# An encoder layer on one core: where the second part of x is loaded and rounded, and when the last half's seven-product sums are added

## The chip, the cores and the metric

The kernel runs on one core of a Trainium2 chip. A core has five engines that run side by side, each through its own list of instructions in order: TensorE (PE, matrix products into the eight banks of PSUM), VectorE (DVE), ScalarE (ACT), GpSimd (POOL) and SyncE (SP, which here only starts transfers). They wait for each other through semaphores. The metric is the device time of one execution in microseconds; the kernel before has a median of 1289.85 us over 3 runs (1289.42 to 1290.4).

## The reference

One layer over 256 positions of width 2048, in float32: a token mixer of two gated branches, a convolutional gated MLP, a last RMSNorm. What matters here is the first projection and the last one:

```python
def mixer_block(x, g_norm, w_in, ln_g, ln_b, w_s, b_s, rpb, w_branch, w_out):
    h = rms_norm(x, g_norm)
    proj = h @ w_in
...
    merged = g_a * (y_a @ w_branch[:GM_WIDTH]) + g_b * (y_b @ w_branch[GM_WIDTH:])
    return x + merged @ w_out

def conv_ffn(x, g_norm, w_up, conv_k, conv_b, w_down):
    h = rms_norm(x, g_norm)
    up = h @ w_up
...
    gate, val = jnp.split(up, 2, axis=-1)
    return x + (jax.nn.silu(gate) * val) @ w_down
...
        x = conv_ffn(x, norm_ffn[l], w_up[l], conv_k[l], conv_b[l], w_down[l])
    return rms_norm(x, norm_final)
```

with w_in 2048 x 9216, w_up 2048 x 11008 and w_down 5504 x 2048.

## The kernel before

**Products in three parts.** Each operand of a product is split into a rounded high part and the rest: ACT rounds (`whi` for weights, L170), DVE subtracts (`wlo`, L171). A product is then three matmuls, high by high, low by high and high by low (L317, L318, L319 in `triple`).

**Pieces.** The weights are streamed as a list of pieces through one queue of SP. `begin(i)` (L197) stands ahead of the matmuls of piece i: it starts loads up to piece i + 4 (LOAD_AHEAD is 5), runs the tasks that were set for piece i with `at(i, ...)`, and issues the split of pieces up to i + 3 (SPLIT_AHEAD is 3, with four buffers for `whi` and four for `wlo`). In the first nine pieces the tasks come before the splits, later behind them. What stands in the engines' lists, and in which order, follows from this. `preload[i]` holds transfers that are started ahead of the load of piece i.

**The start.** The first product is a `wide` group, v = x @ w_in with 1024 columns: a piece holds 128 rows of the weight, in two halves of 512 columns, and goes with one of the sixteen parts of the transposed x (`xr`, 128 x 256 each, made into high and low by `x_split`, L554). Pieces 0, 1 and 2 go with parts 0, 1 and 6 of x. Before the first weights are there, PE runs WAKE matmuls on a tile of ones (L498), whose result nobody reads. Parts 0 and 1 of x are started on ACT's own queue (L477, L478), everything else on SP's. Piece 0 is loaded and split by halves, and the split of part 1 of x stands between its two halves (L181 to L183).

**The end.** The last product, a @ w_down, is made in two halves of 1024 columns, `g_dn[0]` and `g_dn[1]`, each a `wide` group of 43 pieces (numbered 0 to 42 here within the half). In 13 pairs of pieces a scheme with seven products in place of eight is used; four of its results stand in banks of their own, p1, p5, p6, p7, and the other four banks C belong to the output's blocks (t, c), t the half of the positions and c the 512 columns. The last such pair of the second half are pieces 36 and 37. Behind piece 37 `ev_sums` sets two tasks: `first_half` (one ACT copy, L995, and five DVE additions, L996 to L1000, that make the sums and read the four banks) for piece 38, and `second_half` (three DVE additions, L1003 to L1005, into `x2`, the residual) for piece 39. Piece 38 is done in all four blocks; pieces 39 to 42 are done block by block (L440), so that the first blocks can be finished while PE works on the others. When a block is done, `finish` (L1149) runs: DVE adds it to `x2` (L1114), ACT squares and sums it (L1120), DVE multiplies by the norm's weight (L1160). Behind block (0,0), DVE also adds `x2` into the bank of block (1,1) (L1166), ahead of PE's four pieces for that block. When both blocks of a t are there, DVE and ACT make the inverse root (L1174 to L1178), scale the row block (L1186, L1191) and SP and ACT write it out (L1182).

Of the kernel before, what the change touches and what calls it, by code (L numbers as in the profile page):

```python
# [38 lines left out]

LOAD_AHEAD = 5  # L40
SPLIT_AHEAD = 3
WAKE = 9
V_QUADS, V_ORDER = ((5,), (0, 1, 6, 7, 8, 9, 10, 11, 12, 13, 2, 3, 4, 5, 14, 15))
VA_QUADS, VA_ORDER = ((2, 4, 6), (6, 7, 0, 1, 2, 3, 10, 11, 4, 5, 14, 15, 12, 13, 8, 9))
X_TURN = ((0, 0), (3, 1), (4, 2), (5, 3), (1, 4), (2, 5), (6, 6), (7, 9))
# [33 lines left out]
def trunk_kernel(ctx, tc, x, x_t, vecs, w_in, ln_g, ln_b, w_st, b_s, rpb, w_branch, w_out, w_up, w_down,  # L79
                 norm_final, out):  # L80
    nc = tc.nc
# [77 lines left out]
    def split_to(n):  # L159
        while n_split[0] < min(n, len(pieces)):  # L160
            i = n_split[0]
            n_split[0] += 1
            src, r0, kn, (c0, cn, nb, cs), step = pieces[i]
            w = raw.pop(i)
            h = wpool.tile([128, 2, 512], F32R, name="whi", bufs=SPLIT_AHEAD + 1)
            l = wpool.tile([128, 2, 512], F32R, name="wlo", bufs=SPLIT_AHEAD + 1)
            m = cn * nb

            def part(k):
                nc.scalar.activation(h[:, k, :m], w[:, k, :m], AF.Copy)  # L170
                nc.vector.tensor_sub(l[:, k, :m], w[:, k, :m], h[:, k, :m].bitcast(F32))  # L171

            if i in units:
                part(slice(0, units[i]))
            elif i == 1:
                part(slice(0, 1))
                part(slice(1, 2))
            elif i:
                part(slice(0, kn))
            else:  # L180
                part(slice(0, 1))  # L181
                x_split(1)
                part(slice(1, 2))  # L183
            split_t[i] = (h, l)

    tasks = {}
    preload = {}

    def at(i, f):
        tasks.setdefault(i, []).append(f)  # L190
# [6 lines left out]
    def begin(i):  # L197
        cur[0] = i
        load_to(i + LOAD_AHEAD)
        if i < len(SPLIT_TO):  # L200
            run_tasks(i)
            split_to(SPLIT_TO[i])
        else:
            split_to(i + SPLIT_AHEAD + 1)
            run_tasks(i)
# [78 lines left out]
    def wide(src, row0, order, c0, acts, quads, room, done, sums=None, stored=None, split=None, late=False, lead=4, behind=()):  # L284
        n0 = plan_wide(src, row0, order, c0)
        boxes = {}
        for q in quads:
            i = n0 + 2 * q
            k = order[2 * q]
            units[i], units[i + 1] = 1, 2  # L290
            b = boxes[q] = {}
            ready = split[0].get(k // 2) if split else None
            if stored:
                b["acts"] = {}
                at(i - (ready[0] if ready else lead), lambda b=b, k=k: stored(k // 2, b["acts"]))
            else:
                b["acts"] = sums[k]
            if ready:
                halved.add(i)
                for n, lead in zip(("13", "24"), ready[-2:]):  # L300
                    at(i - lead, lambda b=b, k=k, n=n: split[1](k // 2, b, n))
                continue
            whole[i] = whole[i + 1] = None
            halves = late and q == quads[0]
            at(i - 3, lambda i=i, b=b, halves=halves: weight_sums(i, b, room, halves))
            if halves:
                at(i - 2, lambda b=b: b.pop("rest")())
            at(i - (1 if q in behind else 2), lambda b=b: weight_sums_split(b, room))
        return ("wide", n0, order, acts, quads, boxes, done)
# [160 lines left out]
    def load_xt(k, n, queue=None):  # L470
        c = slice(KD + k * T if k else 0, KD + (k + n) * T)
        (queue or nc.sync).dma_start(xall[:, c], x_t[:, c])
# [2 lines left out]
    gffn = const.tile([128, KD], F32)  # L475
    ck = const.tile([128, 4, 2 * NF], F32)
    load_xt(0, 1, nc.scalar)  # L477
    load_xt(1, 1, nc.scalar)  # L478

    def load_late():  # L480
        nc.sync.dma_start(gffn, vecs[:, :KD])
# [14 lines left out]
    def keep_awake(n):  # L496
        for _ in range(n):
            nc.tensor.matmul(wake, idle[:, :128], idle[:, :512], start=True, stop=True)  # L498

    keep_awake(WAKE)  # L500

# [52 lines left out]
    def x_split(k):  # L554
        a, g = xT[k], gmix[:, k:k + 1]
        if k:
            nc.scalar.activation(a[:, 0, :], xr[:, k], AF.Copy, scale=g)
        else:
            nc.vector.tensor_scalar(a[:, 0, :], xr[:, k], g, None, op0=OP.mult)
        nc.vector.scalar_tensor_tensor(a[:, 1, :], xr[:, k], g, a[:, 0, :].bitcast(F32), op0=OP.mult, op1=OP.subtract)  # L560
# [8 lines left out]
    def first_room(name, dt):  # L569
        return ypool.tile([128, 2, 512], dt, name=f"y{first_rooms.index('t13' if name == 'f' else name)}")  # L570
# [411 lines left out]

    rs = {}

    def ev_sums(j, room):
        def done(P, i):
            x2 = rs["x2"]
            p1, p5, p6, p7 = P
            x11, x12, x21, x22 = (x2[:, t, c * 512:(c + 1) * 512] for t in range(2) for c in (j, j + 1))
            m = {}  # L990

            def first_half():
                ab, cd = room("t13", F32), room("t24", F32)
                m["v"], m["u3"], m["w"] = cd[:, 0], cd[:, 1], ab[:, 0]
                nc.scalar.activation(ab[:, 0], p1, AF.Copy)  # L995
                nc.vector.tensor_add(x11, p1, x11)  # L996
                nc.vector.tensor_sub(ab[:, 1], ab[:, 0], p6)
                nc.vector.tensor_add(m["v"], p5, ab[:, 1])
                nc.vector.tensor_add(m["u3"], p7, ab[:, 1])
                nc.vector.tensor_add(m["w"], p5, m["u3"])  # L1000

            def second_half():
                nc.vector.tensor_sub(x12, x12, m["v"])  # L1003
                nc.vector.tensor_add(x21, x21, m["u3"])
                nc.vector.tensor_sub(x22, x22, m["w"])  # L1005

            at(i + 1, first_half)
            at(i + 2, second_half)
        return done


# [221 lines left out]
    for n, (q, i, j) in enumerate(X_SUMS):  # L1233
        sum_acts_at(i, j, first_sums[2 * q], lambda q=q: q,
                    lambda name, dt, i=i: first_room("s2" if name == "f" and i < 16 else name, dt), f"s{n}", True)
# [17 lines left out]
    def split_read(kept, g, tile_of, queue=nc.gpsimd):  # L1253
        def read(pair, box, n):
            u = box.setdefault("u", [])
            u.append([tile_of(pair, p + n) for p in "hl"])
            for t, src in zip(u[-1], kept[pair, g][n]):
                queue.dma_start(t.bitcast(F32), src)
            if len(u) == 2:
                split_sums(box, u)  # L1260
        return read
# [62 lines left out]
    def out_split_tile(pair, name):  # L1324
        if pair == OUT_SET:
# [3 lines left out]
    t_kept = {}  # L1329
    g_o = [wide(w_o, 0, OUT_ORDER[g], g * 1024, lambda k: mg["mT"][k], OUT_QUADS[g], sums_room,  # L1330
                (ev_sums(2 * g, sums_room), ev_out(g)), m_sums, split=(OUT_SPLIT[g], split_read(t_kept, g, out_split_tile)), late=g == 0) for g in range(2)]
    dram = keep("dram", space=bass.MemoryType.DRAM)
    for n, (pair, g) in enumerate((pair, g) for g in range(2) for pair in OUT_SPLIT[g]):
        t_kept[pair, g] = split_rows("out", pair, g)
        i = g_at[2 * n][1]
# [46 lines left out]
    for n, q in enumerate(OUT_PAIRS):  # L1382
        i = g_m2[0][1] + OUT_SUMS[n]
# [22 lines left out]
    def down_order(g):  # L1406
        free = [p for p in range(NF // 2) if p not in DOWN_PAIRS]
        kept = list(DOWN_PAIRS)
        pairs = [(kept if q in DOWN_QUADS[g] else free).pop(0) for q in range(NF // 2)]
        return tuple(2 * p + kk for p in pairs for kk in range(2)) + (NF - 1,)  # L1410

    g_dn = [wide(w_d, 0, down_order(g), g * 1024, lambda k: ff["a"][k], DOWN_QUADS[g], down_room,
                 (ev_sums(2 * g, down_room), ev_down if g == 0 else finish), stored=stored,
                 split=({p: (6, 6) for p in DOWN_SPLIT}, split_read(d_kept, g, down_split_tile))) for g in range(2)]
    ff["kept"] = {p: dram.tile([128, 2, 512], F32, name=f"sums{p}") for p in DOWN_PAIRS}
    for p, turn in zip(DOWN_SPLIT, DOWN_JOBS):
        for g in range(2):
            d_kept[p, g] = split_rows("down", p, g)
            i = g_up[turn[g]][1]
            split_ahead(w_d, d_kept, lambda: ff["more"], lambda c: "so", nc.gpsimd, p, g, g * 1024, i, range(i + 6, i + 10), (i + 10, i + 12), 0)  # L1420

    first_chunk = X_TURN[1][0]
    preload[2] = [lambda: load_xt(2 * first_chunk, 1)]
    preload[3] = [lambda: load_xt(2 * first_chunk + 1, 1)]
    for n, (c, _) in enumerate(X_TURN[2:]):
        preload.setdefault(n + 4, []).append(lambda c=c: load_xt(2 * c, 2))
    for n, i in enumerate(LOAD_ROWS):
        preload.setdefault(i, []).append(lambda n=n: load_x(512 * n, 512))
    at(0, lambda: x_split(0))
    at(0, lambda: split_to(1))  # L1430
    at(1, lambda: x_split(2 * first_chunk))
    at(1, lambda: split_to(3))
# [165 lines left out]
```

## Time and profile before

| | |
|---|---|
| median of 3 runs | 1289.85 us (1289.42 to 1290.4) |
| the profiled execution's own time | 1290.33 us |
| its span, first to last instruction | 1288.5 us |
| granted TensorE clock, mean over the span | 0.998 |
| DVE busy | 1118.3 us, 87% of the span, 1644 instructions |
| ACT busy | 793.0 us, 62%, 1179 instructions |
| POOL busy | 162.1 us, 13% |
| DMA read and written | 284 GB/s over the span |

Times in a timeline are counted from the span's start. A row gives the start, the duration, the engine, the line, the operation, what it writes and reads, how many such instructions stand in the row, and in brackets how long the engine had been idle before it and what it had waited for. PEld are weight loads into the array, which run beside the matmuls. "SPq" and "ACTq" are the instructions that start transfers. The chain of waits is the sequence of work that ended last, followed back from the end.

### The profile page before, as it was taken

What the parts mean: (1) busy time and instruction counts of PE and PEld (TensorE: products, weight loads), DVE (VectorE), ACT (ScalarE), POOL (GpSimd) and SP (SyncE); (2) the same over time, 40 slices, a digit from 0 to 9 for tenths busy, and PEclk for the clock granted to TensorE, in tenths of its full rate; (3) what the DMA queues carried; (4) which work ended last, traced back from release to release, by engine and by line L of the source; (5) the groups of instructions that cost most, each with busy time, mean ns of one, the idle gap of its engine ahead of it and who ended that gap; (6) DMA issues with size and microseconds to landing.
All of it is one profiled execution on the core that took longest, in us unless ns stands there. A gap on an engine that the chain in (4) does not pass through costs nothing.

```text
span 1288.5 us, 19673 instructions
## 1 busy us (share of the span) xinstructions
PE 1277.2 (99%) x6717; PEld 1088.7 (84%) x6717; DVE 1118.3 (87%) x1644; ACT 793.0 (62%) x1179; POOL 162.1 (13%) x307
## 2 busy tenths in 40 slices
PE   9999999999999999999999999999999999999997
PEld 7888888888887888888888888888888888888885
DVE  7898977777799989996889999998988989979987
ACT  7776575775755655565665666665665656556654
POOL 0003852330000001100001000100000001211210
PEclk9999999999999999999999999999999999999999
DMA  9789889989789977965688789888776859998993
GB/s 364 278 272 284 288 263 345 341 284 321 247 314 360 347 238 262 387 215 179 193 281 286 239 275 304 272 260 291 261 227 219 279 174 359 374 387 321 353 392 132
DMA packets 199893, 369.51 MB, mean 287 GB/s; under 512 B 15984, under 2 KB 124144, under 8 KB 199792
## 3 DMA queue, kind: packets, MB, share of 16 engines
q1 hardware_dynamic: 175472, 286.36, 64.7%
q0 software_dynamic: 23888, 81.23, 17.7%
q8 instruction: 52, 0.85, 0.2%
q10 hardware_dynamic: 432, 0.66, 0.1%
q14 instruction: 49, 0.40, 0.1%
HBM read 320.48 MB, written 45.61 MB: 284 GB/s over the span
## 4 chain that ended last, share of the span: by engine, by line
PE 96%; DVE 2%; DMA 1%; issue 1%; DVEq 0%; ACT 0%; SPq 0%; ACTq 0%
PE bank L222 31%; PE bank L226 16%; PE bank L319 11%; PE bank L317 11%; PE bank L318 11%; PE bank L250 5%; PE bank L251 5%; PE bank L252 5%; DMA wraw<-in_w_down_dram 1%; DVE wlo L171 1%; PE bank L871 0%; PE bank L825 0%; PE bank L498 0%; PE bank L860 0%; PE bank L698 0%
## 5 line engine op out<-in xcount | busy, mean ns | idle before, releaser
L171 DVE TENSOR_TENSOR wlo<-wraw,whi 128x1024 fp32r<-128x1024 f32 (+1 forms) x472 | 537.4, 1152 | 125.0 <-ACT whi L170 74.8
L170 ACT ACTIVATE whi<-wraw 128x1024 fp32r<-128x1024 f32 (+1 forms) x472 | 463.8, 995 | 224.1 <-PE bank L318 65.1
L222 PE MATMUL bank<-h,whi 128*128 128x512 f32 x1760 | 423.3, 391 | 0.0
L222 PEld LDWEIGHTS bank<-h,whi 128*128 128x128 f32 x1760 | 322.7, 188 | 62.1
L226 PEld LDWEIGHTS bank<-h,wlo 128*128 128x128 f32 x1760 | 225.9, 191 | 8.8
L226 PE MATMUL bank<-h,wlo 128*128 128x256 f32 x1760 | 228.6, 283 | 0.0
L1076 ACT ACTIVATE tc<-ta,ck 128x256 f32<-128x256 f32 x86 | 47.1, 595 | 109.8 <-DVE ta L1074 109.8
L319 PE MATMUL bank<-wlo,a 128*128 128x512 f32 x188 | 73.4, 390 | 0.6 <-DVE wlo L171 0.6
L318 PE MATMUL bank<-whi,a 128*128 128x512 f32 x188 | 73.2, 389 | 0.0
L317 PE MATMUL bank<-whi,a 128*128 128x512 f32 x188 | 73.1, 389 | 0.0
L317 PE MATMUL bank<-whi,h 128*128 128x512 f32 x186 | 72.8, 392 | 0.0
L319 PE MATMUL bank<-wlo,h 128*128 128x512 f32 x186 | 72.6, 390 | 0.0
L318 PE MATMUL bank<-whi,h 128*128 128x512 f32 x186 | 72.6, 390 | 0.0
L1079 DVE SCALAR_TENSOR_TENSOR tc<-ta,ck,tc 128x255 f32<-128x255 f32 x86 | 41.4, 482 | 14.4 <-ACT tc L1076 14.4
L250 PE MATMUL bank<-whi,h 128*128 128x512 f32 x128 | 50.3, 393 | 0.0
L250 PE MATMUL bank<-whi,y 128*128 128x512 f32 x128 | 50.3, 393 | 0.0
L251 PE MATMUL bank<-whi,h 128*128 128x512 f32 x128 | 49.8, 389 | 0.0
L251 PE MATMUL bank<-whi,y 128*128 128x512 f32 x128 | 49.8, 389 | 0.0
L252 PE MATMUL bank<-wlo,h 128*128 128x512 f32 x128 | 49.8, 389 | 0.0
L252 PE MATMUL bank<-wlo,y 128*128 128x512 f32 x128 | 49.8, 389 | 0.0
L374 ACT ACTIVATE h<-h 128x1024 fp32r<-128x1024 f32 x36 | 38.1, 1059 | 17.5 <-DVE h L364 12.0
L1308 POOL DMA_DIRECT2D down_h<-so x16 | 8.7, 544 | 311.2 <-ACT tc L1086 184.9
(325 smaller groups left out, 1990.1 us busy)
## 6 DMA issues: line engine op xcount, KB each, us to landing
wraw<-in_w_up_dram SPq DMA_DIRECT2D x336, 256.0 KB, 4.1
wraw<-in_w_in_dram SPq DMA_DIRECT2D x107, 512.0 KB, 6.1
wraw<-in_w_down_dram SPq DMA_DIRECT2D x78, 512.0 KB, 7.5
wraw<-in_w_in_dram SPq DMA_DIRECT2D x70, 256.0 KB, 4.4
wraw<-in_w_branch_dram SPq DMA_DIRECT2D x32, 512.0 KB, 5.3
wraw<-in_w_out_dram SPq DMA_DIRECT2D x28, 512.0 KB, 5.9
h<-sums POOLq DMA_DIRECT2D x18, 512.0 KB, 7.5
tw<-in_w_down_dram POOLq DMA_DIRECT2D x8, 1024.0 KB, 8.9
```

What stands on the lines that cost most here:

```text
L170: nc.scalar.activation(h[:, k, :m], w[:, k, :m], AF.Copy)
L171: nc.vector.tensor_sub(l[:, k, :m], w[:, k, :m], h[:, k, :m].bitcast(F32))
L222: nc.tensor.matmul(p, h[:, k - k0, b * 128:(b + 1) * 128], acts(k), start=k == 0, stop=k == nk - 1)
L226: nc.tensor.matmul(p[:, :T], l[:, k - k0, b * 128:(b + 1) * 128], acts(k)[:, 0, :], start=False, stop=False)
L250: nc.tensor.matmul(p, xh, h[:, kk, :m], start=st, stop=False)
L251: nc.tensor.matmul(p, xl, h[:, kk, :m], start=False, stop=False)
L252: nc.tensor.matmul(p, xh, l[:, kk, :m], start=False, stop=sp)
L317: nc.tensor.matmul(p, xh, h, start=st, stop=False, **kw)
L318: nc.tensor.matmul(p, xl, h, start=False, stop=False, **kw)
L319: nc.tensor.matmul(p, xh, l, start=False, stop=sp, **kw)
L1076: nc.scalar.activation(v, u, AF.Identity, scale=ck[:, 1, ch:ch + 1], bias=ck[:, 3, ch:ch + 1])
L1079: nc.vector.scalar_tensor_tensor(v[:, 1:], u[:, :T - 1], ck[:, 0, ch:ch + 1], v[:, 1:], op0=OP.mult, op1=OP.add)
```

## The change

Four edits. Part 1 of x is no longer started on ACT's queue at the beginning, but on SP's, ahead of the load of piece 1, which is behind the two loads of piece 0. The split of part 1 of x stands behind both halves of piece 0 and no longer between them. PE runs 8 wake matmuls in place of 9. In the second half of the last product, `first_half` and `second_half` are set for one piece later each: 39 and 40 in place of 38 and 39 (`late` is the half's number g, so the first half of the last product stays as it is, and so does the product before it, which uses the default).

```diff
-WAKE = 9
+WAKE = 8
...
                 part(slice(0, 1))
+                part(slice(1, 2))
                 x_split(1)
-                part(slice(1, 2))
...
     load_xt(0, 1, nc.scalar)
-    load_xt(1, 1, nc.scalar)
...
-    def ev_sums(j, room):
+    def ev_sums(j, room, late=0):
...
-            at(i + 1, first_half)
-            at(i + 2, second_half)
+            at(i + 1 + late, first_half)
+            at(i + 2 + late, second_half)
...
-                 (ev_sums(2 * g, down_room), ev_down if g == 0 else finish), stored=stored,
+                 (ev_sums(2 * g, down_room, g), ev_down if g == 0 else finish), stored=stored,
...
+    preload[1] = [lambda: load_xt(1, 1)]
```

From L478 on the changed kernel's lines have numbers that are lower by one, up to its new line near the end.

SP's list of transfers at the start, before the change (`wraw` 128x512 are the halves of piece 0, 128x1024 the later pieces, `xr` the parts of x):

```order
L143 DMA wraw<-in_w_in_dram 128x512 x2
L145 DMA wraw<-in_w_in_dram 128x1024
L472 DMA xr<-in_x_t_dram 128x256
L145 DMA wraw<-in_w_in_dram 128x1024
L472 DMA xr<-in_x_t_dram 128x256
```

and with the change:

```order
L143 DMA wraw<-in_w_in_dram 128x512 x2
L472 DMA xr<-in_x_t_dram 128x256
L145 DMA wraw<-in_w_in_dram 128x1024
L472 DMA xr<-in_x_t_dram 128x256
L145 DMA wraw<-in_w_in_dram 128x1024
L472 DMA xr<-in_x_t_dram 128x256
```

One transfer of x has come in ahead of piece 1, and each later transfer stands one place further back.

ACT's list at the start, before:

```order
L472 DMA xr<-in_x_t_dram 128x272
L472 DMA xr<-in_x_t_dram 128x256
L491 ACT_TABLE_LOAD
L491 ACTIVATE one<-one 128x1
L170 ACTIVATE whi<-wraw 128x512
L557 ACTIVATE h_109<-xr 128x256
L170 ACTIVATE whi<-wraw 128x512 x3
```

and with the change:

```order
L472 DMA xr<-in_x_t_dram 128x272
L490 ACT_TABLE_LOAD
L490 ACTIVATE one<-one 128x1
L170 ACTIVATE whi<-wraw 128x512 x2
L556 ACTIVATE h_107<-xr 128x256
L170 ACTIVATE whi<-wraw 128x512 x2
```

The second half of piece 0 is rounded ahead of part 1 of x (`h_109`, `h_107`), and one transfer less is started here. DVE's list is changed in the same way.

DVE's list at the end, before, from the splits of pieces 38 to 41 to the first block's addition (`x_5315` is the residual `x2`, `h_13182` and `h_13183` the two tiles of the sums):

```order
L171 TENSOR_TENSOR wlo<-wraw,whi 128x1024 x4
L996 TENSOR_TENSOR x_5315<-bank,x_5315 128x512
L997 TENSOR_TENSOR h_13182<-h_13182,bank 128x512
L998 TENSOR_TENSOR h_13183<-bank,h_13182 128x512
L999 TENSOR_TENSOR h_13183<-bank,h_13182 128x512
L1000 TENSOR_TENSOR h_13182<-bank,h_13183 128x512
L171 TENSOR_TENSOR wlo<-wraw,whi 128x1024
L1003 TENSOR_TENSOR x_5315<-x_5315,h_13183 128x512
L1004 TENSOR_TENSOR x_5315<-x_5315,h_13183 128x512
L1005 TENSOR_TENSOR x_5315<-x_5315,h_13182 128x512
L1114 TENSOR_TENSOR x_5315<-bank,x_5315 128x512
```

and with the change:

```order
L171 TENSOR_TENSOR wlo<-wraw,whi 128x1024 x5
L995 TENSOR_TENSOR x_5314<-bank,x_5314 128x512
L996 TENSOR_TENSOR h_13197<-h_13197,bank 128x512
L997 TENSOR_TENSOR h_13198<-bank,h_13197 128x512
L998 TENSOR_TENSOR h_13198<-bank,h_13197 128x512
L999 TENSOR_TENSOR h_13197<-bank,h_13198 128x512
L1002 TENSOR_TENSOR x_5314<-x_5314,h_13198 128x512
L1003 TENSOR_TENSOR x_5314<-x_5314,h_13198 128x512
L1004 TENSOR_TENSOR x_5314<-x_5314,h_13197 128x512
L1113 TENSOR_TENSOR x_5314<-bank,x_5314 128x512
```

The split of the last piece, 42, stood between the two groups of additions; now it is the fifth of the splits, and all eight additions stand behind it. ACT's list changes alike: the rounding of piece 42 now stands ahead of the copy of `first_half`. Nothing else in the lists of DVE, ACT, POOL and SP differs; on PE only the one wake matmul is gone.

## The prediction, made before the changed kernel was run

> **What bounds the kernel now.** I read the busy times first, then the chain of waits, then the timelines of its two ends, since all four edits are there.
>
> ```profile
> PE 1277.2 (99%) x6717; PEld 1088.7 (84%) x6717; DVE 1118.3 (87%) x1644; ACT 793.0 (62%) x1179; POOL 162.1 (13%) x307
> PE 96%; DVE 2%; DMA 1%; issue 1%; DVEq 0%; ACT 0%; SPq 0%; ACTq 0%
> ```
>
> PE is busy for 99% of the span and is 96% of the chain. Between the ends there is nothing that these edits touch, so the whole change is worth what it does in the first 12 us and in the last 27. At the start (PE rows, then the chain's own pieces):
>
> ```profile
> 1.46 4.02 PE L498 MATMUL bank<-h 128*128 128x512 bf16 x9 [1.46 <-DVE one L488]
> 5.06 0.85 PE L317 MATMUL bank<-whi,h 128*128 128x512 f32 x1
> 6.13 0.55 PE L319 MATMUL bank<-wlo,h 128*128 128x512 f32 x1
> 6.52 0.40 PE L317 MATMUL bank<-whi,h 128*128 128x512 f32 x1
> 6.75 0.39 PE L318 MATMUL bank<-whi,h 128*128 128x512 f32 x1
> ...
> 5.47 0.43 PE bank L317
> 5.90 0.43 PE bank L318
> 11.90 0.38 PE bank L319
> ```
>
> The chain runs from the wake matmuls into the product without a gap: at the front PE waits for its own wake work. It works at 0.43 us per matmul until about 6.5 us and at 0.23 afterwards (6.52 to 6.75).
>
> **The wake matmul and the loads.** One wake matmul is 4.02 / 9 = 0.45 us. What the first product needs, and what it waits for a little later (the last row is a stretch of time: busy us of PE, PEld, DVE, ACT and POOL, the granted clock, the DMA engines' busy share, GB/s):
>
> ```profile
> 4.37 0.63 ACT L170 ACTIVATE whi<-wraw 128x512 fp32r<-128x512 f32 x1 [1.21 <-DMA wraw<-in_w_in_dram]
> 4.53 0.35 DVE L559 TENSOR_SCALAR h<-xr 128x256 fp32r<-128x256 f32 x1 [3.12 <-DMA xr<-in_x_t_dram]
> 5.32 0.68 DVE L171 TENSOR_TENSOR wlo<-wraw,whi 128x512 fp32r<-128x512 f32 x1
> 5.99 1.92 ACT L170 ACTIVATE whi<-wraw 128x512 fp32r<-128x512 f32 x3
> 7.21 0.39 PE L317 MATMUL bank<-whi,h 128*128 128x512 f32 x1
> 8.57 0.39 PE L317 MATMUL bank<-whi,h 128*128 128x512 f32 x1
> 9.40 1.06 ACT L170 ACTIVATE whi<-wraw 128x1024 fp32r<-128x1024 f32 x1 [0.74 <-DMA wraw<-in_w_in_dram]
> 10.50 1.23 DVE L171 TENSOR_TENSOR wlo<-wraw,whi 128x1024 fp32r<-128x1024 f32 x1 [1.31 <-ACT whi L170]
> 11.78 0.19 PEld L319 LDWEIGHTS bank<-wlo,h 128*128 128x128 f32 x1 [0.30 <-DVE wlo L171]
> 2.11 0.43 SPq L472 DMA_DIRECT2D xr<-in_x_t_dram  x1
> 5.00:12.00 7.00, 7.00 (x29) 5.34 (x28) 5.45 (x9) 5.12 (x9) 0.00 (x0) 1.00 0.97 361
> ```
>
> With 8 wakes the first L317 could start 0.45 earlier, and its inputs just about allow it (`whi` is there at 4.37 + 0.63 = 5.00, x at 4.53 + 0.35 = 4.88). But the third matmul needs `wlo`, ready at 5.32 + 0.68 = 6.00, and it started at 6.13: PE gains 0.13 us and then waits. DVE's row waited 3.12 us for x part 0, which keeps its own place at the head of ACT's queue, so I do not move 6.00. Next, piece 2: its load lands at 9.40, `wlo` is done at 10.50 + 1.23 = 11.73, and the weight load of the third matmul already waits 0.30 us for it. Whatever PE gains before 11.78 is added to that wait. So what decides is whether piece 2 lands earlier. It stands one transfer later on SP (0.43 us of issue, the row at 2.11), but as many bytes are ahead of it as before, and the engines of DMA are 97% busy from 5 to 12 us at 361 GB/s: the landing is set by bytes. **Head: 0**, between -0.45 (all inputs earlier by the wake) and +0.43 (piece 2 later by the issue); 0 because the row at 11.78 is the one that ends last.
>
> The swapped roundings cost nothing here: the second half of piece 0 is used at 7.21, part 1 of x and piece 1 at 8.57. Before, ACT was done with the second half at 5.99 + 1.92 / 3 = 6.63 and with piece 1 at 5.99 + 1.92 = 7.91; the same four roundings in another order end there too, and part 1 of x lands ahead of piece 1, which follows it in SP's queue. That cover is 0.66 us; beyond it each late microsecond is one of PE's. The bound of +0.43 covers it.
>
> On the same place the Trainium skill speaks against the edit: "Trainium Kernel Development and Optimization", section Key Constraints, says that transfers started from several queues share the same 16 engines, and that only issue time is saved. By that rule the move to SP loses the saved issue, up to the +0.43 of my bound, and wins no bandwidth; the 97% row agrees with shared engines, and no row here shows two queues faster than one.
>
> **The end: the sums behind the last split.** Rows of DVE, ACT and PE:
>
> ```profile
> 1268.15 1.06 ACT L170 ACTIVATE whi<-wraw 128x1024 fp32r<-128x1024 f32 x1 [3.62 <-PE bank L318]
> ...
> 1266.94 0.69 DVE L996 TENSOR_TENSOR x<-bank,x 128x512 f32<-128x512 f32 x1
> 1270.19 1.22 DVE L171 TENSOR_TENSOR wlo<-wraw,whi 128x1024 fp32r<-128x1024 f32 x1
> 1271.32 0.69 DVE L1003 TENSOR_TENSOR x<-x,h 128x512 f32<-128x512 f32 x1
> 1273.13 0.69 DVE L1114 TENSOR_TENSOR x<-bank,x 128x512 f32<-128x512 f32 x1
> 1274.46 0.69 DVE L1166 TENSOR_TENSOR bank<-bank,x 128x512 f32<-128x512 f32 x1
> 1279.14 0.75 DVE L1186 TENSOR_SCALAR x<-x,b 128x1024 f32<-128x1024 f32 x1
> 1280.98 0.21 DVE L1175 TENSOR_SCALAR a<-ss,part 128x1 f32<-128x1 f32 x1 [0.38 <-ACT junk L1120]
> ...
> 1270.44 0.39 PE L318 MATMUL bank<-whi,a 128*128 128x512 f32 x1
> 1271.46 0.50 PE L319 MATMUL bank<-wlo,a 128*128 128x512 f32 x1 [0.63 <-DVE wlo L171]
> 1277.28 0.39 PE L317 MATMUL bank<-whi,a 128*128 128x512 f32 x1
> ```
>
> Before: DVE does the five additions (1266.94 to 1270.19, 3.25 us), then the split of piece 42 (1.13 us until the next starts), the three additions (1271.32 to 1273.13, 1.81), then `finish`. PE could have had its L319 at 1270.44 + 0.23 = 1270.67 and starts it at 1271.46: 0.79 us lost.
>
> Now: the split of piece 42 comes first. It needs the rounding by ACT, and that row waits not for ACT's turn but for PE: a `whi` buffer comes free when piece 38's matmuls are done. So it still ends at 1268.15 + 1.06 = 1269.21. DVE, free at 1266.94, has eight additions queued behind the waiting split and stands idle for 1269.21 - 1266.94 = 2.27 us. Then the split (1.13), 3.25 and 1.81: `finish` begins at 1275.40 where it began at 1273.13, **2.27 later**. The split is done at 1269.21 + 1.22 = 1270.43, ahead of 1270.67: PE's 0.79 us are won, as the edit's form suggests, and PE would start its last block at 1277.28 - 0.79 = 1276.49. But that block waits for L1166, which has x2 added to its bank: before, it ended at 1274.46 + 0.69 = 1275.15, 2.13 us ahead of PE; now at 1277.42, 0.93 behind it. The win is gone there, and PE ends 0.14 us later than before.
>
> From 1273.13 on DVE's list is a chain in which no row waits for PE; its only wait is 0.38 us ahead of L1175, for ACT's squares of the last block. So the first row block's scaling (L1186 at 1279.14) moves by 2.27, and the last block's, after the 0.38, by 1.89. What that does to the end is read from the transfers:
>
> ```profile
> 1279.92 3.73 SPq L1182 DMA_DIRECT2D out_dram<-x  x5
> 1281.00:1282.00 1.00, 0.00 (x0) 0.00 (x0) 0.79 (x4) 0.27 (x1) 0.00 (x0) 1.00 1.04 410
> 1285.00:1286.00 1.00, 0.00 (x0) 0.00 (x0) 0.00 (x0) 0.00 (x0) 0.00 (x0) 0.50 1.01 382
> 1286.00:1287.00 1.00, 0.00 (x0) 0.00 (x0) 0.00 (x0) 0.00 (x0) 0.00 (x0) 0.50 0.27 97
> ```
>
> The first write is started at 1279.92, right behind L1186, and from 1281 to 1286 the DMA engines are full with the 2 MB of output: a stream that starts 2.27 later and has no holes ends 2.27 later. **End: +2.2**, between 1.9 (the last block alone decides) and 2.6 (2.27 and a slower restart of PE, the 0.50 against 0.39 of the row at 1271.46, on each of the three matmuls of a triple).
>
> **Sum.** 0 + 2.2 on the profiled execution's own 1290.33 us gives 1292.5. The median of the runs is 0.48 below that execution, so the forecast of the median is 1289.85 + 2.2 = 1292.05, rounded 1292.0. The bounds give 1289.85 - 0.45 + 1.9 = 1291.3 and 1289.85 + 0.43 + 2.6 = 1292.9.
>
> **Rivals.** (1) Not slower: the late sums are hidden and only PE's gain shows. It needs the rounding of piece 42 to be done when DVE is free, at 1266.94, so that DVE has no hole; the row's 3.62 us of waiting for PE speaks against it. Even then DVE's chain has as much work, and the end can gain only the 0.38 us ahead of L1175; with the whole wake, 0.38 + 0.45: 1289.0 to 1289.85, about 1289.4. The same time comes out if the edits do nothing that counts. (2) Slower still, at the start: PE's fast rate began 6.52 - 1.46 = 5.06 us after its first wake matmul. If the new hole between the wakes and the product starts this over, PE is slow from 5.06 for another 5.06 us, to 10.1 instead of 6.5: 3.6 us in which it does 3.6 / 0.43 = 8.4 matmuls in place of 15.7, 7.3 x 0.23 = 1.7 us lost, less the 0.30 of waiting that it covers: 1.4 more, 1293.4. It decides from the length of the hole on; with inputs at 5.00 it is some 0.1 to 0.2 us, which speaks against it. The Trainium skill has this gate ("TensorE: Matmul & The Clock Gate", Part 1, What's actually happening): the slow time is a free-running window of about 3.4 us that must be busy, not a count of matmuls. By it a missed window costs half of 3.4 us, an estimate of 1.7, the same rival; the 5.06 us here lie between one window and two, which agrees.
>
> **How the numbers follow.** Forecast 0.82, rival 1 0.12, rival 2 0.06. The runs of before spread by half a microsecond about their median, which widens the forecast's 1291.3 to 1292.9. The range of 1290.0 to 1293.5 holds it and rival 2 and leaves out rival 1. A change of 0.2%, about what can be told from none here, is 2.58 us: 1292.43 and 1287.27. A quarter of the forecast lies above 1292.43 (0.20), with rival 2 0.26; nothing but a surprise gives less than 1287.27 (0.01); same 0.73.
>
> **What would show it.** DVE idle for some 2.3 us ahead of the split of piece 42, that wait ending with ACT's rounding; no wait of PE for that `wlo`; a new wait of PE of about 0.9 us for DVE's L1166 at the last block; the first write some 2.3 us later against the start of piece 38. At the start: 8 wakes, L317 a little before 5.06, and the wait for piece 2's `wlo` still there and longer. Wrong would be: the rounding of piece 42 without a wait for PE, no hole on DVE, or a start of piece 3 that has moved by more than 0.2 us.

## The result and the profile after

The changed kernel took 1293.25 us (median of 9 runs, 1292.76 to 1294.17), the kernel before 1290.10 us (9 runs, 1289.26 to 1291.53): 3.15 us more, a ratio of 1.0027 with a 95% interval of 1.0018 to 1.0036. That is slower; the middle of the interval lies a little above the 0.2% that can be told from no change, its lower end a little below. The profiled execution took 1293.82 us with a span of 1292.0, against 1290.33 and 1288.5.

From the page of the changed kernel, the busy times and the shares of the chain of waits:

```profile
PE 1277.3 (99%) x6716; PEld 1088.0 (84%) x6716; DVE 1117.7 (87%) x1644; ACT 792.6 (61%) x1179; POOL 162.2 (13%) x307
...
PE 96%; DVE 2%; DMA 1%; issue 0%; ACT 0%; SPq 0%; DVEq 0%; ACTq 0%
```

No engine's busy time grew by more than 0.1 us, and the large shares of the chain are the same. The loss is waiting, and all but 0.09 us of it lies at the two ends.

**The start.** PE's rows in the changed kernel: the wake matmuls, the first L317 of pieces 0, 1, the third matmul of piece 2, and the first L317 of piece 3.

```profile
1.45 3.20 PE L497 MATMUL bank<-h 128*128 128x512 bf16 x8 [1.45 <-DVE one L487]
4.93 0.49 PE L317 MATMUL bank<-whi,h 128*128 128x512 f32 x1 [0.28 <-ACT whi L170]
...
8.74 0.50 PE L317 MATMUL bank<-whi,h 128*128 128x512 f32 x1 [0.18 <-ACT whi L170]
...
12.87 0.50 PE L319 MATMUL bank<-wlo,h 128*128 128x512 f32 x1 [0.38 <-DVE wlo L171]
...
15.28 0.39 PE L317 MATMUL bank<-whi,h 128*128 128x512 f32 x1
```

PE starts the product 0.13 us earlier (4.93 for 5.06), has lost that by piece 1 (8.74 for 8.57), and is 1.09 us late at the third matmul of piece 2 (12.87 for 11.78). Before, piece 3 began at:

```profile
14.18 0.39 PE L317 MATMUL bank<-whi,h 128*128 128x512 f32 x1
```

So the start costs 15.28 - 14.18 = **1.10 us** in this pair of executions. Where that comes from is seen on ACT, in the roundings of pieces 0, 1 and 2 of the changed kernel:

```profile
4.25 1.39 ACT L170 ACTIVATE whi<-wraw 128x512 fp32r<-128x512 f32 x2 [1.57 <-DMA wraw<-in_w_in_dram]
...
8.06 1.15 ACT L170 ACTIVATE whi<-wraw 128x512 fp32r<-128x512 f32 x2 [2.02 <-DMA wraw<-in_w_in_dram]
...
10.50 1.06 ACT L170 ACTIVATE whi<-wraw 128x1024 fp32r<-128x1024 f32 x1 [0.74 <-DMA wraw<-in_w_in_dram]
```

Piece 2 is rounded at 10.50 where it was at 9.40: its load landed 1.10 us later, and PE's start of piece 3 is later by the same 1.10. The row at 8.06 is piece 1, and ACT had waited 2.02 us for its load. Piece 1 alone had already made PE late: it began piece 2 at 11.88, before at 11.29, and the wait for piece 2's `wlo` came on top. What the DMA engines did meanwhile is in the last two columns of the windows (busy share, GB/s), first before, then after:

```profile
4.50:6.50 2.00, 2.00 (x6) 1.05 (x5) 1.82 (x4) 1.43 (x3) 0.00 (x0) 1.00 1.04 393
```

```profile
4.50:6.50 2.00, 1.62 (x5) 0.86 (x5) 1.97 (x5) 1.41 (x3) 0.00 (x0) 1.00 0.85 282
6.50:9.00 2.50, 2.31 (x10) 1.57 (x9) 0.68 (x3) 0.94 (x2) 0.00 (x0) 1.00 0.97 361
```

For 2 us the engines are not full any more: (393 - 282) x 2 = 222 KB less is moved. At the 361 GB/s of the next stretch that takes 0.6 us, an estimate that covers a good half of the 1.10. It is not only the transfer that left ACT's queue: SP's own queue moved 0.72 MB in these 2 us before and 0.56 MB now.

**The end.** The mark here is the first matmul of piece 38, before and after:

```profile
1265.46 0.39 PE L317 MATMUL bank<-whi,a 128*128 128x512 f32 x1
```

```profile
1266.65 0.39 PE L317 MATMUL bank<-whi,a 128*128 128x512 f32 x1
```

It came 1.19 us later, so only 0.09 was added between piece 3 and piece 38. From the mark to the end of the span it was 1288.55 - 1265.46 = 23.09 us and is 1292.04 - 1266.65 = 25.39: the end costs **2.30 us**. DVE's rows after (the splits of pieces 38 to 41, the split of 42, the first of the eight additions, `finish`, the addition into the last block's bank, the first row block's scaling):

```profile
1263.32 4.62 DVE L171 TENSOR_TENSOR wlo<-wraw,whi 128x1024 fp32r<-128x1024 f32 x4
1270.44 1.23 DVE L171 TENSOR_TENSOR wlo<-wraw,whi 128x1024 fp32r<-128x1024 f32 x1 [2.50 <-ACT whi L170]
1271.58 0.68 DVE L995 TENSOR_TENSOR x<-bank,x 128x512 f32<-128x512 f32 x1
...
1276.63 0.68 DVE L1113 TENSOR_TENSOR x<-bank,x 128x512 f32<-128x512 f32 x1
...
1277.96 0.69 DVE L1165 TENSOR_TENSOR bank<-bank,x 128x512 f32<-128x512 f32 x1
...
1282.64 0.75 DVE L1185 TENSOR_SCALAR x<-x,b 128x1024 f32<-128x1024 f32 x1
```

DVE stands idle for 2.50 us ahead of the split of piece 42. From there on its list has the work it had before: from the first instruction behind the four splits to `finish` it was 1273.13 - 1266.94 = 6.19 us, and is 1276.63 - 1270.44 = 6.19. The chain of waits says what the hole waits for:

```profile
1269.08 0.24 PE bank L318
1269.35 1.07 ACT whi L170
1270.44 1.23 DVE wlo L171
```

PE's matmul with the old `whi` buffer, then ACT's rounding into it, then DVE's split. And PE itself, by its waits (total, count, longest) and its last block's first matmul:

```profile
PE bank L317 <- DVE bank L1165: 1.0, 1, 1.0
```

```profile
1278.70 0.50 PE L317 MATMUL bank<-whi,a 128*128 128x512 f32 x1 [0.98 <-DVE bank L1165]
```

PE no longer waits for the last `wlo`, but 0.98 us for DVE's addition into the last block's bank. The write stream, and the DMA engines while it runs out:

```profile
1283.41 3.38 SPq L1181 DMA_DIRECT2D out_dram<-x  x5
```

```profile
1288.00:1289.00 1.00, 0.00 (x0) 0.00 (x0) 0.00 (x0) 0.00 (x0) 0.00 (x0) 0.50 1.01 391
1289.00:1290.00 1.00, 0.00 (x0) 0.00 (x0) 0.00 (x0) 0.00 (x0) 0.00 (x0) 0.50 0.68 250
```

It starts 3.49 us later than before (1279.92), which is 1.19 + 2.30, and ends about as much later: the last busy slice was 1286 to 1287 with a share of 0.27, and is 1289 to 1290 with 0.68.

### The profile page after: what moved, and what is told of

It is laid out like the page before. It is cut to its first block, busy times and chain, and to the rows that moved or that the text cites. A ratio compares the mean times of both kernels' runs of the same rounds, so it can differ in the third digit from the quotient of the medians.

```text
span 1292.0 us, 19671 instructions
## 1 busy us (share of the span) xinstructions
PE 1277.3 (99%) x6716; PEld 1088.0 (84%) x6716; DVE 1117.7 (87%) x1644; ACT 792.6 (61%) x1179; POOL 162.2 (13%) x307
## 4 chain that ended last, share of the span: by engine, by line
PE 96%; DVE 2%; DMA 1%; issue 0%; ACT 0%; SPq 0%; DVEq 0%; ACTq 0%
PE bank L222 31%; PE bank L226 16%; PE bank L319 11%; PE bank L318 11%; PE bank L317 11%; PE bank L250 5%; PE bank L251 4%; PE bank L252 4%; DMA wraw<-in_w_in_dram 1%; DVE wlo L171 1%; PE bank L870 0%; PE bank L824 0%; PE bank L859 0%; PE bank L697 0%; PE bank L1049 0%
## 5 line engine op out<-in xcount | busy, mean ns | idle before, releaser
L317 PE MATMUL bank<-whi,a 128*128 128x512 f32 x188 | 73.3, 390 | 1.0 <-DVE bank L1165 1.0
L317 PE MATMUL bank<-whi,h 128*128 128x512 f32 x186 | 72.6, 390 | 0.5 <-ACT whi L170 0.5
```

The lines of the kernel that those rows point to most:

```text
L317: nc.tensor.matmul(p, xh, h, start=st, stop=False, **kw)
```

## The experiments

Two questions were open: how the 3.15 us divide between the four edits, and why the start costs anything. For the end the theory was the hole: DVE's list waits for PE through the `whi` buffer, and all that stands behind it moves. For the start, theory A was that the place of x's part 1 ahead of piece 1 in SP's queue delays the weights; the rivals were the wake matmul, the order of the roundings, and that only the bytes count. Each kernel was timed beside the kernel before on the same chip. The first ten are edits of the kernel before, after_again is the changed kernel itself, and after_x_act is an edit of it; all compute the whole layer.

| kernel | median, runs | before | difference | ratio, 95% interval |
|---|---|---|---|---|
| late_only | 1292.60, 10 | 1290.16 | +2.44 | 1.0020 (1.0011 to 1.0029) |
| head_only | 1290.58, 10 | 1290.16 | +0.42 | 1.0005 (0.9996 to 1.0015) |
| wake_only | 1290.36, 10 | 1290.16 | +0.20 | 1.0002 (0.9993 to 1.0012) |
| x_move_only | 1290.47, 10 | 1290.16 | +0.31 | 1.0004 (0.9994 to 1.0013) |
| order_wake | 1290.08, 10 | 1290.14 | -0.06 | 0.9998 (0.9989 to 1.0007) |
| more_act | 1290.29, 10 | 1290.14 | +0.15 | 0.9999 (0.9990 to 1.0008) |
| x_behind | 1290.45, 10 | 1290.31 | +0.14 | 1.0002 (0.9993 to 1.0011) |
| mid_dve | 1291.16, 11 | 1290.14 | +1.02 | 1.0007 (0.9998 to 1.0016) |
| mid_pool | 1290.64, 11 | 1290.14 | +0.50 | 1.0003 (0.9994 to 1.0011) |
| late_own | 1290.77, 11 | 1290.31 | +0.46 | 1.0003 (0.9994 to 1.0012) |
| after_again | 1293.58, 8 | 1290.20 | +3.38 | 1.0027 (1.0017 to 1.0038) |
| after_x_act | 1292.59, 11 | 1290.20 | +2.39 | 1.0018 (1.0009 to 1.0027) |

**late_only: the end alone.**

```diff
-            at(i + 1, first_half)
-            at(i + 2, second_half)
+            at(i + 1 + late, first_half)
+            at(i + 2 + late, second_half)
...
+                 (ev_sums(2 * g, down_room, g), ev_down if g == 0 else finish), stored=stored,
```

> Before with the late sums alone (the start as before). Theory: the end costs what its trace showed, 2.3 us, whatever the start does: DVE idle about 2.5 us ahead of the split of piece 42, finish (L1114) begins about 9.98 us after the first matmul of piece 38 where it began 7.67 after it before, PE waits about 1 us at L1166; time 2.3 us over before. Rival: part of the end's loss came from the shifted start (other phases of loads), then the end costs less than 1.5 us here.

It was 2.44 us slower. DVE's split of piece 42 and `finish` in its timeline:

```profile
1269.23 1.23 DVE L171 TENSOR_TENSOR wlo<-wraw,whi 128x1024 fp32r<-128x1024 f32 x1 [2.65 <-ACT whi L170]
...
1275.42 0.68 DVE L1114 TENSOR_TENSOR x<-bank,x 128x512 f32<-128x512 f32 x1
```

The hole is 2.65 us, and behind it come the same 1275.42 - 1269.23 = 6.19 us to `finish`, as in the changed kernel. `finish` stands 9.97 us behind piece 38's first matmul, in the changed kernel 9.98. PE waits 1.0 us for L1166. The late sums alone make most of the loss, with the start left as it was.

**head_only: the other three edits.**

```diff
-WAKE = 9
+WAKE = 8
...
+                part(slice(1, 2))
                 x_split(1)
-                part(slice(1, 2))
...
-    load_xt(1, 1, nc.scalar)
...
+    preload[1] = [lambda: load_xt(1, 1)]
```

> The start's three edits alone (part 1 of x on SP's queue, its split behind piece 0, 8 wakes), the sums as before. Theory: the move of the load costs about 1.1 us, because pieces 1 and 2 land later: piece 2's rounding starts near 10.5 us where it started at 9.40, and the third matmul of piece 2 starts near 12.9 instead of 11.8; time 0.7 to 1.2 us over before. Rival: the late landing was chance of one execution; then piece 2's rounding starts at 9.2 to 9.6 here and the time is within 0.3 us of before.

The interval of its +0.42 also holds no change. The 0.7 to 1.2 us of the theory did not come. The roundings of pieces 1 and 2:

```profile
7.92 1.16 ACT L170 ACTIVATE whi<-wraw 128x512 fp32r<-128x512 f32 x2 [1.95 <-DMA wraw<-in_w_in_dram]
...
9.52 1.06 ACT L170 ACTIVATE whi<-wraw 128x1024 fp32r<-128x1024 f32 x1
```

Piece 1 comes as late as in the changed kernel (7.92, there 8.06), but piece 2 only 0.12 us later than before, as the rival had it. Piece 3 starts at 14.46, 0.28 later than before, without a wait for piece 2: that much comes from piece 1.

**wake_only and x_move_only: which of the three.** wake_only is the line with 8 in place of 9; x_move_only is head_only with 9.

> 8 wakes in place of 9 and nothing else. Theory: nothing, within 0.3 us: PE starts up to 0.4 us earlier and waits for piece 2 instead, whose rounding still starts near 9.4 us. Rival: the hole behind the wakes keeps PE at its slow rate, then the matmuls stand 0.43 us apart beyond 6.5 us and the time is 0.5 to 1.5 us over before.

> The load of part 1 of x moved to SP's queue and its split behind both halves of piece 0, with 9 wakes. Theory: this carries the whole loss of the start: piece 1's first rounding near 8.0 us and piece 2's near 10.5 (before 6.6 and 9.4), time 0.7 to 1.2 us over before, like the run with all three edits of the start. Rival: the wakes or chance; then it is within 0.3 us of before.

By time neither can be told from before (+0.20 and +0.31), so here too the 0.7 to 1.2 us expected of the move did not come. By profile they differ: piece 1 is rounded at 7.03 with 8 wakes alone, as in late_only, which leaves the start alone (6.92), and at 7.71 with the moved load, after 1.61 us of waiting for it. It is the moved load that delays piece 1, not the wake.

**order_wake and x_behind: the place in the queue.** order_wake has 8 wakes and the new order of the splits, and leaves the load on ACT's queue. x_behind has it on SP, but one place later, behind piece 1 (9 wakes, new order):

```diff
...
-    load_xt(1, 1, nc.scalar)
...
-    preload[2] = [lambda: load_xt(2 * first_chunk, 1)]
+    preload[2] = [lambda: load_xt(1, 1), lambda: load_xt(2 * first_chunk, 1)]
```

> Before with 8 wakes and the split of part 1 of x behind both halves of piece 0, but its load left on ACT's queue. Theory (the queue is what costs): DMA engines 0.97 or more busy from 4.5 to 6.5 us, piece 1's first rounding near 6.7 us, piece 2's near 9.2, time within 0.3 us of before. Rival (the order of the splits costs): piece 1's rounding near 7.9 as in the runs with the moved load, time 0.3 to 0.5 over before.

> The load of part 1 of x on SP's queue, but one place later, behind piece 1, and its split behind both halves of piece 0; 9 wakes. Theory A (a small transfer ahead of piece 1 in its queue delays piece 1): piece 1 lands early again, the DMA engines are 0.97 or more busy from 4.5 to 6.5 us, but part 1 of x lands late; Theory B (all loads in one queue leave holes wherever the small one stands): busy 0.85 to 0.92 from 4.5 to 6.5 us, as in the runs with the load ahead of piece 1. By both the time is 0 to 0.6 us over before.

Differences of -0.06 and +0.14. The roundings of pieces 1 and 2 and the window of x_behind:

```profile
7.17 1.14 ACT L170 ACTIVATE whi<-wraw 128x512 fp32r<-128x512 f32 x2
...
9.63 1.06 ACT L170 ACTIVATE whi<-wraw 128x1024 fp32r<-128x1024 f32 x1 [0.74 <-DMA wraw<-in_w_in_dram]
```

```profile
4.50:6.50 2.00, 1.90 (x7) 0.97 (x6) 1.82 (x4) 0.87 (x2) 0.00 (x0) 1.00 0.99 357
```

Behind piece 1 the same transfer in the same queue leaves the engines full (0.99), and ACT doesn't wait for piece 1's load; it waits for part 1 of x instead, 1.28 us. order_wake has 1.02 there and piece 1 at 6.83. So no cost of the order of the splits or of the wake is seen, and the delay of piece 1 belongs to the place ahead of it, as theory A said. In time these starts differ by less than their intervals.

**more_act: still more of x on ACT's queue**, parts 6 and 7 too.

```diff
     load_xt(1, 1, nc.scalar)
+    load_xt(6, 1, nc.scalar)
+    load_xt(7, 1, nc.scalar)
...
-    preload[2] = [lambda: load_xt(2 * first_chunk, 1)]
-    preload[3] = [lambda: load_xt(2 * first_chunk + 1, 1)]
```

> Before with parts 6 and 7 of x also started on ACT's queue at the beginning, so that SP's queue holds weights alone there. Theory (small transfers in SP's queue leave holes, a second queue fills them): DMA engines 1.0 busy from 4.5 to 6.5 us, piece 1's and piece 2's rounding at 6.7 and 9.2 or earlier; time 0 to 0.4 us below before. Rival (only bytes count): pieces 1 and 2 land later, since parts 6 and 7 now take their share ahead of them: piece 1's rounding 0.3 to 0.7 us later, time the same or up to 0.4 over.

No difference (+0.15); the DMA share from 4.5 to 6.5 us is 1.02, piece 1 is rounded at 7.13, piece 2 at 9.60. Moving more transfers off SP's queue doesn't bring the weights earlier, as the rival had it for engines that are full; the moved load of the change is another case because it leaves them not full.

**after_again and after_x_act: the same question in the changed kernel.** after_again is the changed kernel itself; after_x_act puts the load back on ACT's queue.

```diff
     load_xt(0, 1, nc.scalar)
+    load_xt(1, 1, nc.scalar)
...
-    preload[1] = [lambda: load_xt(1, 1)]
```

> The changed kernel as it is, a second execution with a profile, beside the next run on the same chip. Theory: 2.7 to 3.3 us over before; piece 1's first rounding at 7.5 us or later and the DMA engines 0.92 or less busy from 4.5 to 6.5 us again, but piece 2's landing scatters (9.5 to 10.5 us), and the 1.2 us that the start lost in the first profile is at the upper end of what it costs (0.3 to 1.2). Rival: the start always loses 1.1 us or more in this kernel.

> The changed kernel with the load of part 1 of x put back on ACT's queue; the late sums, 8 wakes and the new order of the splits stay. Theory: only the end's loss is left, 2.3 to 2.5 us over before and 0.3 to 0.9 us below the changed kernel; the DMA engines 0.97 or more busy from 4.5 to 6.5 us. Rival (the queue is nothing in this kernel): within 0.2 us of the changed kernel.

1293.58 against 1292.59: the load's queue is worth 0.99 us here. The table's intervals, some 1.2 us to either side, are against the kernel before and not for this pair; but of the 11 runs of after_x_act only one (1293.43) lies above the fastest of after_again (1293.19). What is left, +2.39, is what late_only lost. Piece 2 was late in this second execution too, where it had been expected to scatter. Piece 2's rounding in after_again, and the windows of after_again and of after_x_act:

```profile
10.41 1.06 ACT L170 ACTIVATE whi<-wraw 128x1024 fp32r<-128x1024 f32 x1 [0.74 <-DMA wraw<-in_w_in_dram]
```

```profile
4.50:6.50 2.00, 2.00 (x6) 1.06 (x5) 1.96 (x5) 1.39 (x3) 0.00 (x0) 1.00 0.83 283
```

```profile
4.50:6.50 2.00, 2.00 (x6) 1.07 (x4) 1.71 (x4) 1.37 (x3) 0.00 (x0) 1.00 1.01 366
```

The low share goes with the moved load and comes again in the second execution. Piece 1's rounding in before is the second in a row of three (5.99 + 1.92 / 3 = 6.63). Over the profiles, the start of piece 3 follows piece 2's rounding:

| kernel | piece 1 rounded | piece 2 rounded | piece 3 starts | piece 3 less piece 2's rounding | DMA share, 4.5 to 6.5 us |
|---|---|---|---|---|---|
| order_wake | 6.83 | 9.13 | 13.89 | 4.76 | 1.02 |
| before | 6.63 | 9.40 | 14.18 | 4.78 | 1.04 |
| wake_only | 7.03 | 9.28 | 14.09 | 4.81 | 1.04 |
| late_only | 6.92 | 8.89 | 14.25 | 5.36 | 0.98 |
| after_x_act | 7.32 | 8.92 | 14.21 | 5.29 | 1.01 |
| more_act | 7.13 | 9.60 | 14.39 | 4.79 | 1.02 |
| x_behind | 7.17 | 9.63 | 14.44 | 4.81 | 0.99 |
| head_only | 7.92 | 9.52 | 14.46 | 4.94 | 0.90 |
| x_move_only | 7.71 | 9.70 | 14.47 | 4.77 | 0.91 |
| after_again | 8.05 | 10.41 | 15.18 | 4.77 | 0.83 |
| after | 8.06 | 10.50 | 15.28 | 4.78 | 0.85 |

Where piece 2 comes late, PE follows it at 4.76 to 4.81 us; where it comes before 9 us, PE's own work sets piece 3, at 14.2. In head_only (4.94) it is PE's own work too, made late by piece 1. The moved load gives a low share and a late piece 1 four times out of four. A late piece 2 it gave in both executions of the changed kernel, and hardly in the two of head_only and x_move_only, though head_only's lists at the start are those of the changed kernel. Why a transfer of 128 KB ahead of one of 512 KB leaves the engines not full, and what makes piece 2 late in the one kernel and not in the other, stays open.

**mid_dve and mid_pool: the end without the hole.** The sums are cut: the copy and the first three additions stay with piece 38, the others go behind the split of piece 42. In mid_dve DVE does the last three (`x2`), in mid_pool POOL.

```diff
-            def first_half():
+            def first_part():
...
                 nc.vector.tensor_add(m["v"], p5, ab[:, 1])
-                nc.vector.tensor_add(m["u3"], p7, ab[:, 1])
-                nc.vector.tensor_add(m["w"], p5, m["u3"])
...
+            def second_part():
+                nc.vector.tensor_add(m["u3"], p7, m["ab"][:, 1])
+                nc.vector.tensor_add(m["w"], p5, m["u3"])
...
+            at(i + 1, first_part)
+            if late:
+                at(i + 2, second_part)
+                at(i + 2, lambda: second_half(nc.vector))
...
```

> Before, with the last half's sums cut in two: the ACT copy and three DVE additions stay at piece 38, the other two move behind the split of piece 42, the last three additions stay at the end. Theory (the hole on DVE decides the end, not PE's wait): the hole ahead of that split is about 0.4 us instead of 2.5, PE waits neither for the split nor at L1166, finish begins 0.3 us later than before against piece 38; time within 0.4 us of before although PE wins its 0.8 us. Rival (PE's wait decides): 0.5 to 0.8 us faster than before.

> The same with the last three additions (x2 and the sums, none reads PSUM) on POOL, which is idle there. Theory: DVE's list is shorter by 1.8 us ahead of finish, so finish begins 1.2 to 1.5 us earlier than before against piece 38, the first write starts that much earlier and the time is 0.6 to 1.3 us below before. Rival: POOL's additions take over 1.5 us each, or DVE waits for POOL at L1160, then nothing is gained.

mid_dve, the split of piece 42 and `finish`:

```profile
1269.17 1.23 DVE L171 TENSOR_TENSOR wlo<-wraw,whi 128x1024 fp32r<-128x1024 f32 x1
...
1273.44 0.68 DVE L1121 TENSOR_TENSOR x<-bank,x 128x512 f32<-128x512 f32 x1
```

No hole, no wait of PE for `wlo` or for the bank, and PE's last matmul starts 13.39 us after piece 38's first, where it was 14.31. Still it isn't faster (+1.02, an interval that just holds no change): PE's 0.92 us are worth nothing, since DVE's list sets the end; `finish` stands 8.06 us behind piece 38's first matmul, 0.39 more than before. The median is further above before than the 0.4 us expected, and the profiled execution (1290.64) does not show where the rest goes. mid_pool, rows of DVE and then of POOL:

```profile
1269.38 2.00 DVE L171 TENSOR_TENSOR wlo<-wraw,whi 128x1024 fp32r<-128x1024 f32 x1 [0.53 <-ACT whi L170]
...
1274.63 0.69 DVE L1167 TENSOR_TENSOR h<-x,gfin 128x512 f32<-128x512 f32 x1 [1.34 <-POOL x L1007]
```

```profile
1269.00 1.29 POOL L1005 TENSOR_TENSOR x<-x,h 128x512 f32<-128x512 f32 x1 [22.55 <-DVE h L998]
```

POOL takes 1.29 us for an addition that DVE does in 0.68, DVE's split beside it takes 2.00 in place of 1.22, and DVE then waits 1.34 for POOL. The three additions saved (1.81 us) are given back, by the second half of the rival. The Trainium skill ("GPSIMD Engine Reference", section Specifications) says that POOL's way to SBUF is shared with VectorE and contends with its instructions that have two SBUF inputs; the split has two, and the 2.00 agrees.

**late_own: the late sums without the buffer that makes the hole.** Piece 42 gets a `whi` and a `wlo` tile of its own (tiles of the seven-product scheme that are free by then), so that its rounding needn't wait for piece 38.

```diff
+            if i in own:
+                h, l = own[i]()
+            else:
...
+    own[len(pieces) - 1] = lambda: (down_room("h13", F32R), down_room("l13", F32R))
```

> The late sums, the start as before, and piece 42 split into two tiles of its own (two that the last pair, pieces 36 and 37, has done with), so that its rounding does not wait for the matmuls of piece 38. Theory: no hole on DVE ahead of that split (under 0.3 us), finish begins 7.7 us after piece 38's first matmul as before the change and not 10.0, PE wins its 0.8 us and does not wait at L1166, the time is 0 to 0.4 us below before, 2.0 us or more below the late sums alone. Rival (the late sums are costly by themselves, as work that comes later): finish begins over 9 us after piece 38, time 1.5 us or more over before.

DVE's rows for the split of piece 42 and `finish`:

```profile
1267.46 1.21 DVE L174 TENSOR_TENSOR h<-wraw,h 128x1024 fp32r<-128x1024 f32 x1
...
1273.64 0.68 DVE L1117 TENSOR_TENSOR x<-bank,x 128x512 f32<-128x512 f32 x1
```

The hole is gone, `finish` comes 1273.64 - 1267.46 = 6.18 us after the first instruction behind the four splits, as before, and of late_only's +2.44 there is +0.46 left, within its interval. PE has no wait at the end and starts its last matmul 13.37 us after piece 38's first (before 14.31), and again the time isn't lower than before, where up to 0.4 less was expected. This shows the hole as the cause at the end, and that PE's wait there was off the path.

Where DVE's list itself hangs is seen further back. The last row of DVE that waits for a load is an addition over the weights of the last pair, pieces 36 and 37, before and in late_own:

```profile
1257.06 0.69 DVE L364 TENSOR_TENSOR h<-wraw 128x512 f32<-128x512 f32 x1 [1.13 <-DMA wraw<-in_w_down_dram]
```

```profile
1257.57 0.69 DVE L367 TENSOR_TENSOR h<-wraw 128x512 f32<-128x512 f32 x1 [0.42 <-DMA wraw<-in_w_down_dram]
```

| kernel | that row starts | piece 38 starts | `finish` starts | `finish` less that row | `finish` less piece 38 |
|---|---|---|---|---|---|
| before | 1257.06 | 1265.46 | 1273.13 | 16.07 | 7.67 |
| x_move_only | 1257.07 | 1265.83 | 1273.14 | 16.07 | 7.31 |
| head_only | 1257.43 | 1265.88 | 1273.50 | 16.07 | 7.62 |
| late_own | 1257.57 | 1265.55 | 1273.64 | 16.07 | 8.09 |
| late_only | 1256.61 | 1265.45 | 1275.42 | 18.81 | 9.97 |
| after_x_act | 1257.29 | 1266.16 | 1276.13 | 18.84 | 9.97 |
| after_again | 1257.74 | 1266.44 | 1276.42 | 18.68 | 9.98 |
| after | 1257.98 | 1266.65 | 1276.63 | 18.65 | 9.98 |

In the first four of these kernels, without the hole, DVE works through from that row to `finish`, and the end follows the load. In the other four, with it, the end follows PE's piece 38. late_own's `finish` is later than before because its load landed later. It also bears on the start: x_move_only has PE at piece 38 0.37 us later than before and `finish` no later, while in the changed kernel PE's lateness comes to the end in full. That can be one reason why the moved load costs less alone (+0.31, +0.42) than in the changed kernel (0.99), beside its later piece 2; it was not tested.

## Why the prediction was off

Direction: it gave "within 0.2%" 0.73, and the kernel is slower by a little more than that (1.0027). The 1293.25 us lie in the range, near its upper end; the forecast was 1292.0. The end was right in its mechanism and nearly in its size; the start was wrong.

**The step that failed: "the landing is set by bytes. Head: 0".** It took the 97% of 5 to 12 us for a property of the transfers, whatever their order. In the changed kernel the share from 4.5 to 6.5 us is 0.85, the landing of piece 2 moves by 1.10 and not by 0 to 0.43, and piece 3 starts 1.10 later, beyond the 0.2 named as the mark of being wrong. after_x_act prices the move of the load at 0.99 us in this kernel. What the runs show in its place: the load ahead of piece 1 leaves the DMA engines less than full and delays piece 1 in all four profiles that have it, and piece 2 in both of the changed kernel; why is open. The place was right: what ends last at the start is the third matmul of piece 2, by its `wlo`. The term alone decided the direction: the forecast stood 0.38 us under the bound of 1292.43. The bound of +0.43 was also too tight for this kernel: it priced one issue, and no row bounded what a full set of engines loses when it is not full. The rule of the Trainium skill that was weighed there ("Trainium Kernel Development and Optimization", section Key Constraints), that a second queue only saves issue time, had the sign right. The 0.43 us of issue by which the prediction priced it are less than half of what after_x_act shows, so for the changed kernel the measurement decides; the +0.42 of head_only would not go beyond it.

**The wake matmul**: right, nothing, but the front was misread: PE did not wait for its wake work alone. The weight load of the first L317 had waited for ACT's rounding already before:

```profile
5.05 0.28 PEld L317 LDWEIGHTS bank<-whi,h 128*128 128x128 f32 x1 [0.49 <-ACT whi L170]
```

With `whi` there at 5.00 the inputs allowed 0.06 us, not 0.45. Eight executions with nine wakes started that L317 at 4.79 to 5.06, the six with eight at 4.87 to 4.94. The 0.13 us won (4.93) were used up by piece 1, and the wait for piece 2's `wlo` was there and longer (0.38 us on PE, 0.30 before on its weight load). wake_only can't be told from before.

**The swapped splits**: right, nothing (order_wake, -0.06). The cover of 0.66 us was gone all the same, by the load: piece 1's rounding began at 8.06 where it was 6.63, and PE waited 0.18 us for it.

**The hole on DVE**: right. 2.27 predicted, 2.50 measured, ended by ACT's rounding, which waited for PE. It was larger because DVE was done with the four splits 0.19 us earlier against piece 38 (1267.94 - 1266.65 = 1.29, before 1.48 by the 1266.94 that the prediction took); the rounding ended where the prediction had it, 3.76 us behind piece 38's first matmul (before 3.75).

**`finish` later by 2.27**: 1276.63 - 1266.65 = 9.98 us after piece 38's first matmul, before 7.67, so 2.31. **PE's gain given back**: right, the wait for the bank was 0.98 where 0.93 was predicted. PE's end came 0.37 later against piece 38 and not 0.14, which counted for nothing. **The write stream**: right, 2.30. The end term of +2.2 measured +2.30 in the trace, +2.44 alone. What the prediction did not see is that DVE's list hung on a load before and hangs on PE now.

**The rivals.** Not slower: excluded by the hole. A restart of the slow rate: no such thing; in the changed kernel the matmuls are 0.22 to 0.24 us apart from 6.30 on, as before from 6.52, except at its waits and for steps of 0.34 to 0.39 right behind them.

## What to carry to other kernels

When an instruction is moved ahead in an in-order list, ask what it waits for itself: all that stands behind it inherits that wait, and here the 2.50 us of idle time made the end 2.30 us later. A wait of the busiest engine is worth removing only if that engine sets the end at this place; behind piece 38 it was DVE's list, and mid_dve and late_own, which have no wait of PE there, were no faster. Follow such a list back to its last wait: here that was a load, and the change put PE in its place. And that the transfers are full says where the bound lies with the present order, not that another order of the queue keeps them full.

## What was not expected of the hardware

- A load of 128 KB moved from ACT's queue to SP's, ahead of a load of 512 KB, lowered the DMA engines' share from 4.5 to 6.5 us from 0.98 to 1.04 (six kernels with it on ACT's queue) to 0.83 to 0.91 (four profiles); behind that load it was 0.99. The reason is open.
- POOL's addition of 128x512 f32 took 1.29 us, DVE's 0.68, and DVE's split of 128x1024 beside it 2.00 in place of 1.22.
- The wake matmuls ran at another rate from one execution of the same kernel to the next: eight took 3.20 us in one of the changed kernel and 3.60 in the other. Piece 3 began at 15.28 and 15.18, so it is the loads, not this rate, that set the start here.
